# The first weight blocks of a two-layer trunk: an early constant copy on ScalarE, and no look-ahead for three blocks

## The chip, the cores and the metric

The kernel runs on one core of one Trainium2 chip, in one launch. Its time is the device time of one execution in microseconds; a lower time is better. Five engines take part: TensorE (PE in the profile; its weight loads are PEld), VectorE (DVE), ScalarE (ACT), GpSimd (POOL) and SyncE (SP, whose queue issues nearly all transfers). Host work (laying out arrays) is not in the time.

## What is computed

The reference is a decoder trunk of two layers on 512 tokens of width 1024, in float32. Layer A: a projection, pooling over windows of 2, 4, 8 and 16 positions, a grouped projection, four heads of attention to a memory of 256 tokens, an output projection, and a SwiGLU feed-forward of width 2816. Layer B: the same frame with stick-breaking attention of twelve heads in place of pooling. Only the start matters here:

```
def pool_layer(x, mem, mem_norm, norm_mix, w_in, ...):
    proj = rmsnorm(x, norm_mix) @ w_in
    u_pool, q_mem = proj[..., :POOL_WIDTH], proj[..., POOL_WIDTH:]
    ...
    mk, mv = memory_kv(mem, mem_norm, w_mem_kv)
    mem_out = memory_attention(q_mem, mk, mv)
    x = x + jnp.concatenate([grouped, mem_out], axis=-1) @ w_out
    return x + swiglu(rmsnorm(x, norm_ffn), w_gu, w_down)
```

## The kernel before

Everything is kept feature-major: a tile has 128 features on its partitions and 512 tokens along its free axis, so the residual stream is eight tiles, x0 to x7. To get nearly float32 precision at the fast rate, each operand is split in two: a high part (`xh`, `wh`) that ScalarE rounds to the type fp32r, and a remainder (`xl`, `wl`) that VectorE forms as source minus high part. A product is three matmuls of 128 x 512 into one PSUM accumulator (`mm3`): `wh` by `xh`, `wh` by `xl` and `wl` by `xh`. The norm's gain is folded into the weights: `wsplit` lets ScalarE write `wh` as weight times gain, and VectorE form `wl`.

Weights come as a stream of blocks ("bricks") of 128 x 512 in a planned order. The generator `bricks` yields them one by one, split, and starts a transfer whenever a new chunk begins. A chunk is two blocks (512 KB). Only the very first chunk is fetched as two transfers of 256 KB, with the fetch of x0 between them. `next_brick` hands the next block to a product, and keeps a queue `ahead` of up to `AHEAD` = 2 further blocks that have already been issued to the engines. One block is put into that queue before the first product is set up:

```
    net.first = lambda: fetch_x(0)
    net.ahead.append(next(net.feed))
```

The first product is the first half of the input projection (`a_in`): eight blocks, k = 0 to 7, each used for four accumulators, 12 matmuls a block. At each block `mul_in` calls `x_at(k)`, which issues the fetch of the tile x(k+1) (at k = 3: of all that remain) and the split of x(k). So what the program's order puts ahead of what on ScalarE, VectorE and the SyncE queue depends on how far `next_brick` has run ahead. The tile framework's scheduler works from that order. For the first half of the input projection it orders TensorE as well; from the memory projection on TensorE's order is fixed by hand (`in_order`).

Ahead of everything stand 20 transposes of a constant (`warm`, line 149), which occupy TensorE until data is there. The norm's statistics are squares on ScalarE (`sq`, `ssq`), sums on VectorE, and a small product `ps_ss` on TensorE; its result comes back as a row `bc` that TensorE transposes into `ps_bc`. The accumulators are first read after that.

Of the kernel before, what the change touches and what calls it, by code (L numbers as in the profile page):

```python
# [13 lines left out]
AF = mybir.ActivationFunctionType  # L14
# [46 lines left out]
AHEAD = 2  # L61
# [62 lines left out]
class Net:  # L124
    def __init__(self, ctx, tc, a, out):
        self.ctx, self.tc, self.nc, self.a, self.out = ctx, tc, tc.nc, a, out
        nc = self.nc
        self.const = ctx.enter_context(tc.tile_pool(name="const", bufs=1))
        self.wp = ctx.enter_context(tc.tile_pool(name="wp", bufs=4))
        self.tp = ctx.enter_context(tc.tile_pool(name="tp", bufs=1))  # L130
        self.pp = ctx.enter_context(tc.tile_pool(name="pp", bufs=1, space=PSUM))
        self.turn = 0
        self.now = 0.0
        self.when = {}
        self.free = {"act": 0.0, "dve": 0.0, "sp": 0.0}
        self.sides = ()
        self.banks = [0.0] * (8 - NACC)
        self.accs = deque([0.0] * NACC)
        self.gains = self.const.tile([P, 7 * KD + 6], F32, name="gains")
        nc.scalar.dma_start(self.gains, a["gains"])  # L140
        self.ident = self.const.tile([P, P], F32, name="ident")
        make_identity(nc, self.ident)
        self.ones = self.const.tile([P, 1], F32, name="ones")
        nc.gpsimd.memset(self.ones, 1.0)
        self.mhalf = self.const.tile([P, 4], F32, name="mhalf")
        nc.gpsimd.memset(self.mhalf, -0.5)
        warm = self.ps("warm")
        for i in range(WARM):
            nc.tensor.transpose(warm[:, (i % 4) * P:(i % 4 + 1) * P], self.ident, self.ident)
        self.feed, self.ahead = self.bricks(), []  # L150
        self.xh = [None] * KD
        self.xl = [None] * KD

# [42 lines left out]

    def next_brick(self, name):

        while len(self.ahead) <= AHEAD:
            nxt = next(self.feed, None)  # L200
            if nxt is None:
                break
            self.ahead.append(nxt)
        got, parts = self.ahead.pop(0)
        assert got == name
        return parts
# [893 lines left out]
```

## Time and profile before

| | us |
|---|---|
| median of three runs | 1110.95 (1109.68 to 1111.78) |
| the profiled execution, its own time | 1112.74 |
| its span, first to last instruction | 1111.0 |
| TensorE busy in the span | 1088.5 (98%) |
| VectorE busy | 677.2 (61%) |
| ScalarE busy | 498.1 (45%) |
| GpSimd busy | 77.4 (7%) |

All moments below are counted from the start of the span. Busy time of TensorE is the time in which at least one matmul is under way; a matmul's own duration (about 0.39 us for 128 x 512) is longer than the distance to the next one's start, since they are pipelined. A row of the timeline merges neighbours of one kind: start, total length, engine, line, tiles, count, and in brackets the idle time of the engine just before and what ended it.

### The profile page before, as it was taken

Reading aid. Unit: us, or ns where it says so; the run is one execution under the profiler, and the core shown is the slowest. Engines: PE = TensorE matmul, PEld = TensorE weight load, DVE = VectorE, ACT = ScalarE, POOL = GpSimd, SP = SyncE. Lnnn points to the kernel's source line nnn. Section 1 sums busy time; section 2 is a strip of 40 time slices with the busy share of each in tenths; the row PEclk is TensorE's granted clock in tenths of the full one; section 3 lists DMA queues with packets and bytes.
Section 4 is the critical chain, followed back from the end, with each engine's and each line's share of the span. In section 5 each row is a group of like instructions: output and inputs, shape, how many; then the busy total and the mean of one; then the engine's idle time right before and its main releaser. Section 6 shows DMA issues by size and latency. Waiting matters only on the chain.

```text
span 1111.0 us, 14383 instructions
## 1 busy us (share of the span) xinstructions
PE 1088.5 (98%) x5280; PEld 914.1 (82%) x5280; DVE 677.2 (61%) x1118; ACT 498.1 (45%) x911; POOL 77.4 (7%) x126
## 2 busy tenths in 40 slices
PE   9999999999999999999998999999999999999997
PEld 7987888888888888888877888778888888888887
DVE  7987766543454534565578799884563365435574
ACT  7558444332333323344786677553332243323343
POOL 0000120000000000000013143340000000000000
PEclk9999999999999999999998999999999999999999
DMA  7463222222222223223554534122222223222212
GB/s 270 140 196 103 95 94 93 99 95 95 95 95 95 97 101 104 98 95 97 135 148 111 132 100 115 58 76 95 95 96 96 99 95 107 97 95 95 95 57 76
DMA packets 39366, 117.48 MB, mean 106 GB/s; under 512 B 5120, under 2 KB 7168, under 8 KB 39296
## 3 DMA queue, kind: packets, MB, share of 16 engines
q1 hardware_dynamic: 39152, 116.54, 32.5%
q8 instruction: 41, 0.67, 0.3%
q14 instruction: 29, 0.24, 0.1%
q10 hardware_dynamic: 144, 0.03, 0.0%
HBM read 100.83 MB, written 2.10 MB: 93 GB/s over the span
## 4 chain that ended last, share of the span: by engine, by line
PE 89%; ACT 3%; DVE 3%; issue 2%; DMA 1%; POOL 0%; SPq 0%; POOLq 0%; DVEq 0%; ACTq 0%
PE acc L274 27%; PE acc L275 27%; PE acc L276 27%; PE av L646 2%; PE tp L557 1%; ACT pt L588 1%; PE zs L607 1%; PE zs L606 1%; DVE wl L224 1%; DMA wr_a_in<-in_a_in_dram 1%; ACT wh L223 1%; ACT pt L593 1%; PE ps_ss L298 0%; PE last L274 0%; PE last L275 0%
## 5 line engine op out<-in xcount | busy, mean ns | idle before, releaser
L274 PE MATMUL acc<-xh,wh 128*128 128x512 f32 x880 | 343.0, 392 | 2.0 <-DVE vs L548 1.1
L275 PE MATMUL acc<-xl,wh 128*128 128x512 f32 x880 | 343.0, 390 | 0.0
L276 PE MATMUL acc<-xh,wl 128*128 128x512 f32 x880 | 342.3, 390 | 0.0
L274 PEld LDWEIGHTS acc<-xh,wh 128*128 128x128 f32 x880 | 165.5, 188 | 35.7 <-ACT xh L233 1.7
L276 PEld LDWEIGHTS acc<-xh,wl 128*128 128x128 f32 x880 | 165.3, 188 | 34.9
L275 PEld LDWEIGHTS acc<-xl,wh 128*128 128x128 f32 x880 | 165.5, 188 | 32.9 <-DVE xl L234 0.2
L224 DVE SCALAR_TENSOR_TENSOR wl<-wr_a_gu,gains,wh 128x512 fp32r<-128x512 f32 x88 | 66.9, 761 | 110.8 <-ACT wh L223 110.8
L224 DVE SCALAR_TENSOR_TENSOR wl<-wr_b_gu,gains,wh 128x512 fp32r<-128x512 f32 x88 | 66.9, 761 | 105.5 <-ACT wh L223 105.5
L223 ACT ACTIVATE wh<-wr_a_gu,gains 128x512 fp32r<-128x512 f32 x88 | 63.7, 725 | 138.8 <-PE acc L275 111.7
L274 PE MATMUL acc<-hh,wh 128*128 128x512 f32 x320 | 124.5, 389 | 0.0
L275 PE MATMUL acc<-hl,wh 128*128 128x512 f32 x320 | 124.5, 389 | 0.0
L276 PE MATMUL acc<-hh,wl 128*128 128x512 f32 x320 | 124.3, 389 | 0.0
L223 ACT ACTIVATE wh<-wr_b_gu,gains 128x512 fp32r<-128x512 f32 x88 | 63.7, 725 | 133.3 <-PE acc L275 105.5
L276 PEld LDWEIGHTS acc<-hh,wl 128*128 128x128 f32 x320 | 60.1, 188 | 12.6
L275 PEld LDWEIGHTS acc<-hl,wh 128*128 128x128 f32 x320 | 60.1, 188 | 12.4
L274 PEld LDWEIGHTS acc<-hh,wh 128*128 128x128 f32 x320 | 60.1, 188 | 12.4
L220 DVE TENSOR_TENSOR wl<-wr_a_down,wh 128x512 fp32r<-128x512 f32 x44 | 30.4, 690 | 60.0 <-ACT wh L219 49.9
L219 ACT CAST wh<-wr_a_down 128x512 fp32r<-128x512 f32 x44 | 27.4, 623 | 72.5 <-PE acc L275 65.4
L303 POOL TENSOR_TENSOR rs<-var,mhalf 128x4 f32<-128x4 f32 (+1 forms) x7 | 6.6, 944 | 758.5 <-DVE var L301 758.5
L220 DVE TENSOR_TENSOR wl<-wr_b_down,wh 128x512 fp32r<-128x512 f32 x36 | 24.9, 690 | 49.1 <-ACT wh L219 40.9
L274 PE MATMUL acc<-mixh,wh 128*128 128x512 f32 x128 | 51.3, 401 | 1.0 <-ACT mixh L994 0.7
L275 PE MATMUL acc<-mixl,wh 128*128 128x512 f32 x128 | 50.1, 391 | 0.2 <-DVE mixl L995 0.2
(198 smaller groups left out, 1695.4 us busy)
## 6 DMA issues: line engine op xcount, KB each, us to landing
wr_a_gu<-in_a_gu_dram SPq DMA_DIRECT2D x44, 512.0 KB, 3.4
wr_b_gu<-in_b_gu_dram SPq DMA_DIRECT2D x44, 512.0 KB, 3.4
wr_a_down<-in_a_down_dram SPq DMA_DIRECT2D x22, 512.0 KB, 3.4
wr_b_qkv<-in_b_qkv_dram SPq DMA_DIRECT2D x20, 512.0 KB, 3.5
wr_b_down<-in_b_down_dram SPq DMA_DIRECT2D x18, 512.0 KB, 3.4
wr_a_out<-in_a_out_dram SPq DMA_DIRECT2D x8, 512.0 KB, 3.5
wr_b_out<-in_b_out_dram SPq DMA_DIRECT2D x8, 512.0 KB, 3.5
wr_a_in<-in_a_in_dram SPq DMA_DIRECT2D x7, 512.0 KB, 4.3
```

Of the source, the lines that this page charges most:

```text
L219: nc.scalar.copy(wh, w)
L220: nc.vector.tensor_tensor(out=wl, in0=w, in1=wh.bitcast(F32), op=ALU.subtract)
L223: nc.scalar.activation(wh[:, c0:c1], w[:, c0:c1], AF.Copy, scale=self.gain(g, k))
L224: nc.vector.scalar_tensor_tensor(out=wl[:, c0:c1], in0=w[:, c0:c1], scalar=self.gain(g, k), in1=wh.bitcast(F32)[:, c0:c1], op0=ALU.mult, o ...
L274: mm(ps, wh, xh, start=first, stop=False)
L275: mm(ps, wh, xl, start=False, stop=False)
L276: mm(ps, wl, xh, start=False, stop=last)
L557: nc.tensor.transpose(tp[:, i * P:(i + 1) * P], blk, self.ident)
L588: nc.scalar.activation(pt[:, b], z[:, b], AF.Exp, scale=sp[:, 2 * pr + i:2 * pr + i + 1], bias=mx[:, i:i + 1], accum_out=sm[:, i:i + 1])
L593: nc.scalar.activation(pt[:, b], pt[:, b], AF.Copy, scale=sm[:, i:i + 1])
L606: nc.tensor.matmul(z[:, :end], q, kh[:, :end], start=True, stop=False)
L646: self.nc.tensor.matmul(to, vv, part, start=ia == 0 and i == 0, stop=ia == nu - 1 and i == len(parts) - 1)
```

## The change

ScalarE gets one instruction more, at the front: it writes a tile of 128 x 1 as 0 times the constant `ones`. And the queue of blocks is not filled ahead for the first three calls: the condition is that one block is in hand until three have been taken, and two more after that.

```
--- before.py
+++ after.py
@@ -144,10 +144,12 @@
         nc.gpsimd.memset(self.ones, 1.0)
         self.mhalf = self.const.tile([P, 4], F32, name="mhalf")
         nc.gpsimd.memset(self.mhalf, -0.5)
+        zero = self.small("zero", 1)
+        nc.scalar.activation(zero, self.ones, AF.Copy, scale=0.0)
         warm = self.ps("warm")
...
-        self.feed, self.ahead = self.bricks(), []
+        self.feed, self.ahead, self.taken = self.bricks(), [], 0
...
     def next_brick(self, name):
 
-        while len(self.ahead) <= AHEAD:
+        self.taken += 1
+        while len(self.ahead) <= (AHEAD if self.taken > 3 else 0):
             nxt = next(self.feed, None)
```

In the built program this is what stands on ScalarE at its front. Names are tile<-source, with buffer numbers: `wr_a_in_0`, `_1`, `_2` are the chunks 0, 1, 2 of the input projection's weights (blocks 0 and 1, 2 and 3, 4 and 5). `xin` is a raw x tile. Before:

```order
L140 DMA gains_67<-in_gains_dram 128x62
L223 ACT_TABLE_LOAD
L223 ACTIVATE wh_107<-wr_a_in_0_102,gains_67 128x512
L233 CAST xh_127<-xin_104 128x512
L283 ACTIVATE ssq_143<-xin_104 128x512
L223 ACTIVATE wh_115<-wr_a_in_0_102,gains_67 128x512
L223 ACTIVATE wh_121<-wr_a_in_1_119,gains_67 128x512
L223 ACTIVATE wh_145<-wr_a_in_1_119,gains_67 128x512
L233 CAST xh_151<-xin_125 128x512
L283 ACTIVATE sq_167<-xin_125 128x512
```

And the same place in the changed kernel:

```order
L140 DMA gains_67<-in_gains_dram 128x62
L148 ACT_TABLE_LOAD
L148 ACTIVATE zero_78<-ones_74 128x1
L226 ACTIVATE wh_109<-wr_a_in_0_104,gains_67 128x512
L236 CAST xh_119<-xin_106 128x512
L286 ACTIVATE ssq_135<-xin_106 128x512
L226 ACTIVATE wh_137<-wr_a_in_0_104,gains_67 128x512
L236 CAST xh_143<-xin_117 128x512
L286 ACTIVATE sq_159<-xin_117 128x512
L286 ACTIVATE sq_186<-xin_141 128x512
L236 CAST xh_170<-xin_141 128x512
L226 ACTIVATE wh_164<-wr_a_in_1_162,gains_67 128x512
```

The activation table is loaded for the new instruction, which needs no transfer, and no longer for the first weight split. The two splits of chunk 1 have moved from ahead of the cast of x1 to behind the cast of x2.

The SyncE queue's transfers at its front, before:

```order
L189 DMA wr_a_in_0_102<-in_a_in_dram 128x512
L847 DMA xin_104<-in_x_dram 128x512
L189 DMA wr_a_in_0_102<-in_a_in_dram 128x512
L193 DMA wr_a_in_1_119<-in_a_in_dram 128x1024
L847 DMA xin_125<-in_x_dram 128x512
L847 DMA xin_149<-in_x_dram 128x512
L193 DMA wr_a_in_2_170<-in_a_in_dram 128x1024
L847 DMA xin_176<-in_x_dram 128x512
```

And in the changed kernel:

```order
L191 DMA wr_a_in_0_104<-in_a_in_dram 128x512
L850 DMA xin_106<-in_x_dram 128x512
L191 DMA wr_a_in_0_104<-in_a_in_dram 128x512
L850 DMA xin_117<-in_x_dram 128x512
L850 DMA xin_141<-in_x_dram 128x512
L195 DMA wr_a_in_1_162<-in_a_in_dram 128x1024
L850 DMA xin_168<-in_x_dram 128x512
L195 DMA wr_a_in_2_193<-in_a_in_dram 128x1024
```

Chunk 1 has moved behind the fetches of x1 and x2, and chunk 2 behind that of x3. VectorE's first 32 rows are reordered in the same sense. On TensorE a few matmuls of blocks 2 and 3 change places, and `ps_ss` stands one matmul later. Behind these places all five engines have the same rows as before, in the same order.

## Rows read from the trace of the kernel before

**Rows 1.** The page: the chain that ended last, shares of the span by engine.

```profile
PE 89%; ACT 3%; DVE 3%; issue 2%; DMA 1%; POOL 0%; SPq 0%; POOLq 0%; DVEq 0%; ACTq 0%
```

**Rows 2.** Timeline of TensorE up to the third block's first matmul.

```profile
1.55 4.53 PE L149 MATMUL warm<-ident 128*128 128x128 f32 x20 [1.55 <-POOL ident masks.py:199]
...
6.36 1.34 PE L274 MATMUL acc<-xh,wh 128*128 128x512 f32 x4 [0.28 <-ACT xh L233]
...
9.14 0.39 PE L276 MATMUL acc<-xh,wl 128*128 128x512 f32 x1
10.14 1.20 PE L274 MATMUL acc<-xh,wh 128*128 128x512 f32 x4 [0.61 <-ACT xh L233]
...
13.02 0.39 PE L274 MATMUL acc<-xh,wh 128*128 128x512 f32 x1
```

**Rows 3.** Timeline of ScalarE up to the cast of x1.

```profile
3.78 1.28 ACT L223 ACT_TABLE_LOAD   x1 [3.78 <-DMA wr_a_in<-in_a_in_dram]
...
5.70 0.60 ACT L233 CAST xh<-xin 128x512 fp32r<-128x512 f32 x1
...
8.24 1.34 ACT L223 ACTIVATE wh<-wr_a_in,gains 128x512 fp32r<-128x512 f32 x2 [0.79 <-DMA wr_a_in<-in_a_in_dram]
9.49 0.60 ACT L233 CAST xh<-xin 128x512 fp32r<-128x512 f32 x1
```

**Rows 4.** Timeline of ScalarE's and SyncE's queues: when transfers are issued.

```profile
0.80 0.41 ACTq L140 DMA_DIRECT2D gains<-in_gains_dram  x1
1.25 0.42 SPq L847 DMA_DIRECT2D xin<-in_x_dram  x1
1.72 0.42 SPq L189 DMA_DIRECT2D wr_a_in<-in_a_in_dram  x1
2.19 0.43 SPq L193 DMA_DIRECT2D wr_a_in<-in_a_in_dram  x1
2.66 0.91 SPq L847 DMA_DIRECT2D xin<-in_x_dram  x2
```

**Rows 5.** Transfers issued 0.80 to 3.61, in order: KB, us to landing.

```profile
gains<-in_gains_dram ACTq DMA_DIRECT2D x1, 31.0 KB, 3.1
...
xin<-in_x_dram SPq DMA_DIRECT2D x1, 256.0 KB, 3.7
...
wr_a_in<-in_a_in_dram SPq DMA_DIRECT2D x1, 256.0 KB, 3.9
...
xin<-in_x_dram SPq DMA_DIRECT2D x1, 256.0 KB, 6.2
...
xin<-in_x_dram SPq DMA_DIRECT2D x1, 256.0 KB, 6.8
...
wr_a_in<-in_a_in_dram SPq DMA_DIRECT2D x1, 512.0 KB, 7.6
```

**Rows 6.** Stretches: us, busy PE, PEld, DVE, ACT, POOL, PEclk, DMA, GB/s.

```profile
13.02:63.49 50.47, 50.47 (x278) 44.02 (x277) 45.44 (x90) 29.79 (x55) 2.16 (x2) 1.00 0.55 186
64.00:100.00 36.00, 32.67 (x209) 28.71 (x208) 33.05 (x72) 29.58 (x70) 0.00 (x0) 1.00 0.52 152
```

**Rows 7.** Timelines of VectorE and TensorE around the statistics.

```profile
22.51 0.69 DVE L287 TENSOR_TENSOR ssq<-ssq,sq 128x512 f32<-128x512 f32 x1
...
26.39 0.95 PE L298 MATMUL ps_ss<-ones,ssq 128*128 128x1 f32 x8
...
28.75 0.43 DVE L305 COPY bc<-rs 128x512 f32<-128x512 f32 x1 [1.21 <-POOL rs L303]
...
30.30 0.60 PE L316 MATMUL ps_bc<-ident,bc 128*128 128x128 f32 x4
30.65 0.36 PE L274 MATMUL acck<-memh,wh 128*128 128x256 f32 x1
```

**Rows 8.** TensorE's timeline at its longest stall, and the stretch around it.

```profile
598.13 0.69 PE L606 MATMUL zs<-kh,qs 128*128 128x384 f32 x1 [3.00 <-DVE atl L234]
...
597.00:605.00 8.00, 6.87 (x30) 6.51 (x31) 5.70 (x11) 4.23 (x11) 1.79 (x4) 0.57 0.44 120
```

## The prediction

> **What bounds the kernel now.** I read the page first: TensorE holds 89% of the chain that ended last [rows 1]. So an edit on ScalarE and on the order of transfers can only pay where TensorE stands still. TensorE's timeline shows where that is at the start [rows 2]. The 20 constant transposes begin at 1.55, and each has its successor 0.216 us behind it (20 of them in 4.53 us, the last 0.42 us long, so the last starts at 5.66). TensorE could take the next matmul at 5.88. It takes the first real one at 6.36, when the cast of x0 has ended (5.70 + 0.60 = 6.30) [rows 3]. The first block's twelfth matmul starts at 9.14, so the block's slot ends at 9.37. The second block starts only at 10.14, again behind a cast, that of x1 (9.49 + 0.60 = 10.09) [rows 2, 3]. The third block starts at 13.02.
>
> ScalarE's timeline tells why both casts are late [rows 3]. The table load of 1.28 us begins at 3.78, when the first weights have landed, and the weight split and the cast queue behind it. Later, ScalarE waits until 8.24 for chunk 1, does that chunk's two splits in 1.34 us, and only then casts x1. Block 1's own weights are long there by then. They were issued at 1.72 and landed 3.9 us later, at 5.62 [rows 4, 5]. So the program waits for blocks 2 and 3 before it prepares block 1's other operand.
>
> From 13.02 to 63.49 TensorE is busy 50.47 of 50.47 us [rows 6]. What it has gained by 13.02 it can keep, if its operands come as much earlier.
>
> **What the change does, part by part.** *The constant copy.* It adds one 128 x 1 instruction and moves the table load to the front, where ScalarE has nothing to do until 3.78. The copy needs only a constant that GpSimd sets before it makes the operand of the transposes (from 1.55). The load then begins behind ScalarE's one transfer issue (0.80 + 0.41 = 1.21) and ends near 2.5, well before 3.78. The first weight split starts when both its inputs are there: the weights at 3.78, the gains at 0.80 + 3.1 = 3.9 [rows 3 to 5]. It is done by about 4.65. The cast then waits for x0, which lands at 1.25 + 3.7 = 4.95 [rows 4, 5], so it ends near 5.6 and TensorE's transposes (5.88) become the later of the two. Hence the copy's 1.28 us is worth at most 6.36 - 5.88 = 0.48 us on TensorE. If that cover were gone, the cast would set the start at about 5.65.
>
> *What the clock takes back.* The first block takes 3.01 us (6.36 to 9.37). Twelve matmuls at the usual distance of 0.2275 us (from 50.47 us of steady work; a block is 2.73 us) make 2.73. The profile writes a granted clock of 1.00 there, but the transposes' 0.216 us is more than twice the 0.0875 us of the four in `ps_bc` (30.30 to 30.65) [rows 7]. So I read the start as the lower level, 1.2 GHz, and the rise as falling just behind the first real matmul. The 0.48 us that TensorE starts earlier then lie at the lower level and do half the work: minus 0.24 us.
>
> *Blocks 2 and 3 at their turn.* The fetches of x1 and x2 take the queue's slots at 2.19 and 2.66, and chunk 1 goes at about 3.14 [rows 4]. x1 then lands near 6.9: before, chunk 1 took that place and its 512 KB landed 2.6 us behind block 1's weights, so 256 KB take about 1.3 us. From its own row of before (6.2 us from issue) it would land at 8.39 at the latest. The cast takes 0.60 us, and block 1 is due on TensorE at 5.88 + 3.01 + 0.24 = 9.13, so either end is early enough. That removes the stall from 9.37 to 10.14, 0.77 us. It also removes the 0.15 us by which the second block was longer than 2.73 (13.02 - 10.14 = 2.88), since the remainder of x1 came late as well.
>
> *Chunk 1 behind x1 and x2.* This is the transfer that becomes later. The same bytes are ahead of its last one as were ahead of the last one of x2 before, which landed at 3.14 + 6.8 = 9.94 [rows 4, 5]. The longest row for 512 KB (chunk 2, 7.6 us from issue) would make it 10.74. Block 2 is due on TensorE at 9.13 + 2.73 = 11.86, and its split takes 0.72, so chunk 1 costs nothing up to 11.1. Behind the waiting split on ScalarE stand the other split, the cast of x3 and block 4's split, due from 14.6 on; they wait with it. Chunk 2 and the x tiles behind it keep their place to within one slot.
>
> *The statistics.* The last sum ends at 23.20 and `ps_ss` is issued at 26.39, so 3.2 us are spare; it now comes one matmul later and 1.2 us earlier. `bc` ends at 29.18 and `ps_bc` is issued at 30.30, with 1.1 us spare, of which the later place takes 0.23 [rows 7]. I count nothing for either.
>
> **Sum.** 0.48 - 0.24 + 0.77 + 0.15 = 1.16 us. Bounds: with the rise of the clock ahead of 5.88, blocks 0 and 1 would take 24 x 0.2275 = 5.46 us from 5.88, so block 2 would start at 11.34, 1.68 earlier; the lower bound is the second rival's 0.5. From 64 to 100 TensorE is idle 3.3 of 36 us [rows 6], in waits on ScalarE and VectorE that themselves start from TensorE's products, so I let that stretch move as a whole. The profiled execution took 1112.74 with a span of 1111.0; it should become 1111.6 and 1109.8. The median, 1.79 lower than the profiled one, becomes 1110.95 - 1.16 = **1109.8**, or 0.10% less. That is below 0.2% (2.2 us), about what a measurement of this kernel can tell from no change.
>
> **Rivals.** *1. The gain is gone later.* Some wait past 64 us may not start from TensorE but from a transfer or an engine that keeps its time. Then nothing is left: 1110.95. For it speaks that VectorE is busy 45.4 of 50.5 us ahead of that stretch; against it, that TensorE loses nothing there, so VectorE's work is in time.
>
> *2. The clock rises later than in this execution.* If the whole first block runs at the lower level (0.455 us a matmul, 5.46 us), it ends at 11.34 now and at 11.82 before. Before, x1 is then long there, and the stall that the change removes doesn't exist: only the earlier start remains, 0.48 us, 1110.5. The rows show one rise only. The Trainium skill, "TensorE: Matmul & The Clock Gate", Part 1, has the slow state as the default that activity releases, and says that the moment differs between runs of one kernel; by that, this case would occur in some executions. The rows bear the first half out (slow transposes, fast matmuls), and one execution can't show the second.
>
> *3. A fall of the clock goes away.* TensorE stands still for 3.00 us before 598.13, and the granted clock is 0.57 on average from 597 to 605: it lies at 1.2 GHz for some 6.9 us and costs 3.4 us of full clock [rows 8]. About 0.5 of that falls on the stall itself, so 3.0 us are lost. If the shifted stall no longer brings a fall, the time is 1110.95 - 1.16 - 3.0 = 1106.8. For it: standing still doesn't always bring a fall, since 3.3 us of it between 64 and 100 leave the granted clock at 1.00 [rows 6]. Against it: this stall's length doesn't change, and executions of before may differ in it already.
>
> *4. Slower: chunk 1 is late.* Two fetches of 256 KB now go ahead of it, and it could fall back further among those behind it. Block 2 then stands still, and blocks 3 to 5 are prepared behind it. Each us past 11.1 costs one; past 12.3 the gain is gone, and a landing past 14.5 (11.4 us from issue) makes it 0.2% slower, 1113.2. No row is longer than 7.6.
>
> **Chances.** Forecast (1.0 to 1.7 us gained, 1109.2 to 1110.0) 0.60; rival 1 0.12; rival 2 0.10; rival 3 0.13; rival 4 0.05. Faster by over 0.2% is rival 3 and about a fifth of the forecast, since the three runs of before are 2.1 us apart: 0.25. Slower 0.05, and within 0.2% 0.70. The range leaves out rivals 3 and 4 (0.18) and adds the spread of runs to the rest: 1107.6 to 1111.5.
>
> **What would show it.** In the profile after, the table load should start before 1.6 and no ScalarE idle time end with it. The first real matmul should start near 5.9, the second block near 9.1 and the third near 11.9, with no idle time named ahead of the second. Chunk 1 should land near 9.9, and the first split of it start there. TensorE should be fully busy to about 62.3, and the last moments should lie 1.2 us earlier. I am wrong if x1 or chunk 1 lands late enough to hold blocks 1 or 2, if a new idle row appears on TensorE before 62, or if the granted clock differs around 600.

## The result and the profile after

The change made the kernel slower: 1131.1 us (median of four runs, 1131.05 to 1133.85) against 1110.3 us before, a ratio of 1.0187 with a 95% interval of 1.0174 to 1.0200. The forecast was 1109.8, in a range of 1107.6 to 1111.5.

The profiled execution after has a span of 1132.1 us. At the start it looks much as forecast. These are rows of the timeline after, of ScalarE first and then of TensorE; they answer to [rows 2, 3]:

```profile
1.24 1.28 ACT L148 ACT_TABLE_LOAD   x1 [1.24 <-PEq L1091]
...
4.68 0.61 ACT L236 CAST xh<-xin 128x512 fp32r<-128x512 f32 x1
...
8.85 0.62 ACT L236 CAST xh<-xin 128x512 fp32r<-128x512 f32 x1 [1.92 <-DMA xin<-in_x_dram]
...
5.73 1.99 PE L277 MATMUL acc<-xh,wh 128*128 128x512 f32 x4
...
9.52 0.76 PEld L277 LDWEIGHTS acc<-xh,wh 128*128 128x128 f32 x4 [0.37 <-ACT xh L236]
9.52 1.20 PE L277 MATMUL acc<-xh,wh 128*128 128x512 f32 x4
...
12.42 0.86 PE L277 MATMUL acc<-xh,wh 128*128 128x512 f32 x3
```

The table load is out of the way, the first real matmul starts at 5.73 in place of 6.36, and the third block at 12.42 in place of 13.02. So 0.6 us are won by then. All the same the span is 21.1 us longer. TensorE doesn't stand still for them. Its row on the page after, and the three rows of its largest product:

```profile
PE 1109.7 (98%) x5280; PEld 915.1 (81%) x5280; DVE 677.9 (60%) x1118; ACT 498.9 (44%) x912; POOL 77.6 (7%) x126
...
L277 PE MATMUL acc<-xh,wh 128*128 128x512 f32 x880 | 348.1, 398 | 1.1 <-DVE vs L551 1.1
L278 PE MATMUL acc<-xl,wh 128*128 128x512 f32 x880 | 347.0, 395 | 0.0
L279 PE MATMUL acc<-xh,wl 128*128 128x512 f32 x880 | 346.6, 395 | 0.0
```

TensorE is busy 21.2 us longer with the same 5280 matmuls (1088.5 before), and idle before these products for no longer than then. The reader should see this first: the bound engine has the same work and no more waits, but more busy time. So each piece takes longer. To see how much, count pieces in a stretch where nothing else happens. From 200 to 500 us both kernels run the feed-forward of layer A without a gap. This is that stretch before (first row, 1325 matmuls in 300 us) and after (second row):

```profile
200.00:500.00 300.00, 300.00 (x1325) 248.39 (x1325) 148.87 (x227) 99.16 (x154) 0.00 (x0) 1.00 0.28 97
```

```profile
200.00:500.00 300.00, 300.00 (x1293) 243.21 (x1292) 142.98 (x218) 95.17 (x147) 0.00 (x0) 1.00 0.27 95
```

300 / 1325 is 226.4 ns a matmul, 300 / 1293 is 232.0: 5.6 ns more, or 2.5%, at a granted clock of 1.00 in both. The page counts 3 x (880 + 320 + 128) = 3984 matmuls of 128 x 512 with split weights. 3984 x 5.6 ns is 22.3 us. Less the 0.6 us won at the start, that makes 21.7 us, where the spans differ by 21.1. It looks closer than it is, for the two profiles also differ in TensorE's clock near 600 us. Before, the granted clock was 0.57 from 597 to 605 [rows 8]; after, it was 0.89 in this stretch:

```profile
605.00:620.00 15.00, 11.76 (x71) 10.59 (x70) 12.19 (x22) 10.55 (x23) 4.67 (x10) 0.89 0.50 120
```

That is some 6.9 us at 1.2 GHz before and some 3.3 after, worth some 1.8 us to the profile after. With it the sum is some 19.9 us, and about 1.2 of the 21.1 stay without an account.

Not every matmul is slower. From the view that groups instructions by line and shape, whole span, before:

```profile
L275 PE MATMUL acc<-hl,wh 128*128 128x512 f32 x320 | 124.5, 389 | 0.0
...
L275 PE MATMUL last<-hl,xh 128*128 128x256 f32 x64 | 18.1, 284 | 0.0
...
L275 PE MATMUL acck<-meml,wh 128*128 128x256 f32 x32 | 9.0, 283 | 0.0
...
L607 PE MATMUL zs<-kb,qs 128*128 128x512 f32 x12 | 4.7, 393 | 0.0
```

and after:

```profile
L278 PE MATMUL acc<-hl,wh 128*128 128x512 f32 x320 | 126.3, 395 | 0.0
...
L278 PE MATMUL last<-hl,xh 128*128 128x256 f32 x64 | 18.1, 284 | 0.0
...
L278 PE MATMUL acck<-meml,wh 128*128 128x256 f32 x32 | 9.0, 282 | 0.0
...
L610 PE MATMUL zs<-kb,qs 128*128 128x512 f32 x12 | 4.7, 392 | 0.0
```

The products of 128 x 512 with `wh` or `wl` as weights went from 389 to 395 ns. The scores `zs` and the last block's product `last` didn't change, and both their operands lie in the same memory pool, the work pool. That points to where tiles lie, but it is a hint and no more. `last` is 128 x 256, and products of that length didn't get slower even with `wh` as weights and a work tile as the moving operand (`acck`, 283 and 282 ns). So the loss is one of the 128 x 512 products, and only the 12 matmuls of `zs` speak for the place; the experiments have to decide. In the built programs, `small("zero", 1)` is the first tile of the work pool `tp`. It has four buffers of 32 bytes, so every work tile behind it begins 128 bytes further along its partition: `xh` at byte 68736 in place of 68608, `hh` at 115840 in place of 115712. The weight tiles `wh` and `wl`, in the pool ahead, stay at 35840 and 44032.

### The profile page after: what moved, and what is told of

Read it like the earlier page. It is cut to its first block, busy times and chain, and to the rows that moved or that the text cites. A ratio compares the mean times of both kernels' runs of the same rounds, so it can differ in the third digit from the quotient of the medians.

```text
span 1132.1 us, 14384 instructions
## 1 busy us (share of the span) xinstructions
PE 1109.7 (98%) x5280; PEld 915.1 (81%) x5280; DVE 677.9 (60%) x1118; ACT 498.9 (44%) x912; POOL 77.6 (7%) x126
## 4 chain that ended last, share of the span: by engine, by line
PE 91%; ACT 3%; DVE 2%; issue 2%; DMA 1%; POOL 0%; SPq 0%; POOLq 0%; DVEq 0%; ACTq 0%
PE acc L277 28%; PE acc L279 27%; PE acc L278 27%; PE av L649 2%; PE tp L560 1%; ACT pt L591 1%; PE zs L610 1%; PE zs L609 1%; ACT pt L596 0%; PE ps_ss L301 0%; PE last L277 0%; PE last L278 0%; PE warm L151 0%; PE last L279 0%; PE acck L279 0%
## 5 line engine op out<-in xcount | busy, mean ns | idle before, releaser
L277 PE MATMUL acc<-xh,wh 128*128 128x512 f32 x880 | 348.1, 398 | 1.1 <-DVE vs L551 1.1
L278 PE MATMUL acc<-xl,wh 128*128 128x512 f32 x880 | 347.0, 395 | 0.0
L279 PE MATMUL acc<-xh,wl 128*128 128x512 f32 x880 | 346.6, 395 | 0.0
```

Source lines behind the costliest of these rows:

```text
L277: mm(ps, wh, xh, start=first, stop=False)
L278: mm(ps, wh, xl, start=False, stop=False)
L279: mm(ps, wl, xh, start=False, stop=last)
```

## The experiments

Theory A: the tile's place does it. Theory B: the new order or the earlier start puts TensorE into a slower state. Theory C: the early copy or table load does it. All times are compared with runs of the kernel before on the same chip (1110.2 to 1111.6 in the median).

**The whole change, but no tile moves.** The copy goes into unused bytes behind a constant. The order on all five engines is that of the changed kernel.

```
-        self.mhalf = self.const.tile([P, 4], F32, name="mhalf")
-        nc.gpsimd.memset(self.mhalf, -0.5)
+        self.mhalf = self.const.tile([P, 5], F32, name="mhalf")
+        nc.gpsimd.memset(self.mhalf[:, :4], -0.5)
+        nc.scalar.activation(self.mhalf[:, 4:5], self.ones, AF.Copy, scale=0.0)
...
-        while len(self.ahead) <= AHEAD:
+        self.taken += 1
+        while len(self.ahead) <= (AHEAD if self.taken > 3 else 0):
```

> The whole change, with every engine's instructions in the order of the changed kernel, but the copy is written into 4 unused bytes behind the constant mhalf, so that no tile moves in memory. Theory A (the new tile moves every later work tile by 128 bytes, and that makes the matmuls of 128 x 512 slower by 5 to 6 ns each): the distance between matmuls is back at 227 ns, and the time is 1.0 to 1.7 us below the kernel before, some 1109. Theory B (the new order or the earlier start puts TensorE into a slower state for the whole run): the distance stays at 232 and the time near 1131. Theory C (the early copy or table load does it): the same as B, near 1131.

Measured: 1109.3 us, ratio 0.9985 (0.9975 to 0.9995). The chosen stretch holds 1325 matmuls again:

```profile
200.00:500.00 300.00, 300.00 (x1325) 248.51 (x1324) 149.13 (x228) 99.49 (x155) 0.00 (x0) 1.00 0.29 97
```

B and C fall: order, copy and table load are all there, and the matmuls are fast. The change's own idea gains 0.15%. Its start on TensorE:

```profile
5.73 1.34 PE L276 MATMUL acc<-xh,wh 128*128 128x512 f32 x4
...
8.72 1.07 PE L276 MATMUL acc<-xh,wh 128*128 128x512 f32 x4
...
11.44 0.84 PE L276 MATMUL acc<-xh,wh 128*128 128x512 f32 x3
```

The third block starts 1.58 us earlier than before (13.02), which agrees with the ratio (0.0015 x 1111 = 1.7 us).

**The look-ahead alone.** No copy, no tile.

```
-        while len(self.ahead) <= AHEAD:
+        self.taken += 1
+        while len(self.ahead) <= (AHEAD if self.taken > 3 else 0):
```

> The look-ahead edit alone: no copy, no new tile, every tile where it was before. Theory A: 227 ns, and a gain of 0.4 to 1.2 us, since the table load again stands behind the first weights but the cast of x1 no longer stands behind chunk 1; near 1109.5. Theory B: near 1131. Theory C: near 1110.

Measured: 1110.0 us, ratio 0.9987 (0.9978 to 0.9996), 1325 matmuls in the stretch. So the order alone brings a gain; what the copy adds can't be told from nothing by these times, since the intervals overlap. In the profile the first real matmul stands at 6.45 here and at 5.73 with the copy, the third block at 12.06 and at 11.44. By these rows 0.62 of the 1.58 us at the third block came with the copy.

**The copy alone,** in its own tile.

```
+        zero = self.small("zero", 1)
+        nc.scalar.activation(zero, self.ones, AF.Copy, scale=0.0)
```

> The copy alone with its tile, look-ahead as before: the work tiles stand 128 bytes later. Theory A: 232 ns and near 1131 to 1132, the first product starting near 5.7 us and the second block still waiting behind chunk 1. Theory B: 227 ns and near 1110. Theory C: near 1131.

Measured: 1133.3 us, ratio 1.0199 (1.0184 to 1.0213), 1293 matmuls in the stretch. The slower matmuls come with the copy's line and without the order.

**Neither edit, only bytes.**

```
+        pad = self.tp.tile([P, 32], F32, tag="pad", name="pad", bufs=1)
+        nc.gpsimd.memset(pad, 0.0)
```

> Neither edit: the kernel before with a tile of 128 bytes per partition put at the front of the work pool, which GpSimd fills once and nothing reads. Theory A: 232 ns, some 21 us slower than before, near 1132. Theories B and C: as before, near 1110.

Measured: 1134.9 us, ratio 1.0212 (1.0196 to 1.0228), 1292 matmuls:

```profile
200.00:500.00 300.00, 300.00 (x1292) 243.21 (x1291) 142.82 (x218) 94.16 (x145) 0.00 (x0) 1.00 0.29 95
```

128 bytes that nothing reads cost what the change cost. Theory A stands; the next runs ask what about the place it is.

**The same bytes ahead of weights and work tiles.**

```
+        pad = self.const.tile([P, 32], F32, name="pad")
+        nc.gpsimd.memset(pad, 0.0)
```

> The kernel before with the 128 bytes put ahead of everything that is large: the split weights wh and wl move by 128 bytes too, and their distance to the work tiles is what it was. Theory A1 (what counts is the place of the moving tile itself, a multiple of 512 bytes before and 128 beyond one after): 232 ns, near 1132. Theory A2 (what counts is the distance between the two operands of a matmul): 227 ns, near 1110.

Measured: ratio 1.0005 (0.9993 to 1.0017), and 1325 matmuls:

```profile
200.00:500.00 300.00, 300.00 (x1325) 248.42 (x1324) 148.87 (x227) 99.00 (x154) 0.00 (x0) 1.00 0.29 97
```

All large tiles lie 128 bytes off their old place, and nothing is slower. A1 falls: it isn't the place of the moving tile by itself, but how it lies to the large tiles ahead of it, the weights among them.

**The bytes behind xh and xl.** Ahead of the first `ssq` tile, which follows them in the pool:

```
+        if not hasattr(self, "pad"):
+            self.pad = self.tp.tile([P, 32], F32, tag="pad", name="pad", bufs=1)
+            nc.gpsimd.memset(self.pad, 0.0)
```

> The kernel before with the 128 bytes put behind the tiles xh and xl and ahead of all later work tiles. So xh and xl stay and hh, hl, mixh, mixl and the rest move. Both A1 and A2: matmuls with xh or xl as the moving tile at 227 ns, those with hh, hl, mixh and mixl at 232 or 233; 960 + 384 such matmuls by 5.7 ns are 7.7 us, so near 1118. A third theory, that the whole program gets slower by where it lies, would slow all or none.

Measured: ratio 1.0079 (1.0050 to 1.0108), 1120.1 us, some 2 us more than forecast. The same stretch by line, both sorts of product inside one execution:

```profile
L275 PE MATMUL acc<-xl,wh 128*128 128x512 f32 x275 | 107.0, 389 | 0.0
...
L275 PE MATMUL acc<-hl,wh 128*128 128x512 f32 x162 | 64.0, 395 | 0.0
```

`xl` hasn't moved and is fast, `hl` has and is slow. That excludes every cause that acts on the program as a whole.

**Other distances.** 32 and 64 bytes at the front of the work pool of the kernel before; then 192 and 96 in the kernel of the first experiment, at the same place. This is the edit for 32 bytes; the others differ in the number of columns (16, 48 and 24 in place of 8).

```
+        pad = self.tp.tile([P, 8], F32, tag="pad", name="pad", bufs=1)
+        nc.gpsimd.memset(pad, 0.0)
```

> The kernel before with a tile of 32 bytes at the front of the work pool. If any step off the place of before costs the same, 232 ns and near 1132; if the cost grows with the step, a quarter of 21 us, near 1116; if what counts is a boundary coarser than 32 bytes that a row of 2048 bytes straddles once more, as with 128: near 1132.

> The same with 64 bytes. Near 1132 if any step costs the same, near 1121 if the cost grows with the step, near 1110 if every other step is free.

> The whole change with the copy in the unused bytes (as in the first run) and the work tiles moved by 192 bytes. If the cost goes by the distance between the operands in steps of 64 bytes that repeat each 128, as 64 (9 us) would say, near 1118; if it grows with the distance, above 1131; if there is a better place than the old one, below 1109.

> The same with 96 bytes: near 1135 if every distance that is not a multiple of 64 costs what 32 did (25 us), between 1118 and 1131 if it lies between its neighbours 64 and 128.

| work tiles moved against the weights by | ratio (interval) | matmuls in 200 to 500 us |
|---|---|---|
| 0 (first experiment) | 0.9985 (0.9975 to 0.9995) | 1325 |
| 32 | 1.0227 (1.0197 to 1.0258) | 1288 |
| 64 | 1.0078 (1.0049 to 1.0107) | 1312 |
| 96 | 1.0208 (1.0179 to 1.0238) | 1287 |
| 128 (neither edit) | 1.0212 (1.0196 to 1.0228) | 1292 |
| 192 | 1.0212 (1.0176 to 1.0248) | 1287 |

The rows for 0, 96 and 192 have the change's own gain of 0.15% in their ratio, the others don't; the counts of matmuls can be compared as they are. The cost neither grows with the distance nor is it the same for all, and 192 isn't 64 again, as I had thought possible. None of these places is better than the old one. At 64 bytes the three matmuls of a product differ, in the same stretch:

```profile
L276 PE MATMUL acc<-xh,wh 128*128 128x512 f32 x276 | 108.8, 394 | 0.0
L278 PE MATMUL acc<-xh,wl 128*128 128x512 f32 x277 | 108.6, 392 | 0.0
L277 PE MATMUL acc<-xl,wh 128*128 128x512 f32 x276 | 107.1, 388 | 0.0
```

All three have moving tiles 64 bytes off, against their own weights and against the next ones alike, as `wh` and `wl` both keep their places. So this distance alone doesn't set what one matmul costs.

**The bytes between wh and wl.** To see whether a matmul's own weights count or those that are loaded beside it.

```
+            if not hasattr(self, "pad"):
+                self.pad = self.wp.tile([P, 32], F32, tag="pad", name="pad", bufs=1)
+                nc.gpsimd.memset(self.pad, 0.0)
             wl = self.wp.tile([P, cols], F32R, tag="wl", name="wl", bufs=4)
```

> The kernel before with the 128 bytes put between wh and wl: wl and all work tiles move, wh stays. So the distance of the moving tile to wl is what it was and that to wh is 128 bytes off. TensorE's order is wh by xh, wh by xl, wl by xh. If a matmul is slowed by the place of its own weights, the two with wh are slow (some 232 ns) and the one with wl is at 227: two thirds of 21 us, near 1124. If it is slowed by the load of the next matmul's weights, which runs beside it, wh by xl (whose next weights are wl) is at 227 and the other two are slow: the same time, and other lines. If what counts were the distance of the moving tile to the tiles that ScalarE and VectorE write meanwhile, no third would stand apart.

Measured: ratio 1.0222 (1.0192 to 1.0251), and no third is fast:

```profile
L279 PE MATMUL acc<-xh,wl 128*128 128x512 f32 x280 | 111.3, 397 | 0.0
L278 PE MATMUL acc<-xl,wh 128*128 128x512 f32 x279 | 110.2, 395 | 0.0
L277 PE MATMUL acc<-xh,wh 128*128 128x512 f32 x279 | 109.6, 393 | 0.0
```

Both of my theories for this run fail. In each of the three matmuls either the own weights or the next ones are `wh`, which lies 128 bytes off, so that both might count. But the matmul with `wl`, whose own place fits, is the longest. The outcome is also the one named for the third theory, the tiles that ScalarE and VectorE write meanwhile. The trace of this run speaks against that one. For 1.71 us neither of the two engines runs, as the first row shows (VectorE and ScalarE 0.00), and TensorE goes on as slowly. The other two rows are its first and last start in this time:

```profile
385.41:387.12 1.71, 1.71 (x9) 1.36 (x8) 0.00 (x0) 0.00 (x0) 0.00 (x0) 1.00 0.40 108
```

```profile
385.44 0.39 PE L277 MATMUL acc<-hh,wh 128*128 128x512 f32 x1
...
387.07 0.40 PE L278 MATMUL acc<-hl,wh 128*128 128x512 f32 x1
```

Seven distances take 1.63 us, 233 ns each. It is so in the whole stretch from 200 to 500 us, counted from the starts in the trace: matmuls during which neither engine runs stand 233.3 ns apart, all others 233.3 as well, and those during which no transfer's packet is under way either, again 233.3. So the loss needs no other engine and no transfer. Between own weights and next weights the run settles nothing.

## Why the prediction was wrong

**The step that failed** is the first sentence on the copy: "It adds one 128 x 1 instruction and moves the table load to the front". I costed the instruction and left out that `small("zero", 1)` also takes memory, at the front of the pool in which every moving operand lies. With it fell the sentence under the bound, "What it has gained by 13.02 it can keep": I took each later matmul to last as it did, and every block's length, the 2.73 us, rests on that. The runs showed in its place 5.6 ns more from one matmul of 128 x 512 to the next (226.4 to 232.0), some 22 us over 3984 of them. No rival had this mechanism. Rival 4, the slower one, had a late chunk 1; that isn't what happened, since chunk 1 is issued at 3.14 and lands 7.5 us later, near 10.6, ahead of the 11.1 that I had named as its limit. Rival 1, the gain gone later, came nearest, but looked for a wait where there is none.

Rival 3, the fall of the clock near 600 us, did bear on the profiles, and one of my signs of being wrong (a granted clock that differs there) came true. These rows are of the first experiment and of the last:

```profile
590.00:605.00 15.00, 12.37 (x70) 10.91 (x69) 12.90 (x22) 9.06 (x19) 2.93 (x7) 0.89 0.59 149
```

```profile
590.00:630.00 40.00, 37.66 (x226) 33.05 (x225) 36.17 (x60) 29.24 (x60) 13.97 (x28) 1.00 0.41 107
```

So the time at 1.2 GHz was some 6.9 us in the profile before, some 3.3 in those of the change and of the first experiment, and none in that of the last run. TensorE's longest stall there was 3.0, 3.2, 2.6 and 2.3 us, so its length alone doesn't decide. Whether the change shortens the fall or executions of one kernel differ in it, one profile of each can't say. It explains none of the loss: where the clock is 1.00 throughout, the matmuls are as slow.

**What was right, by the steps at the start.** *The copy* frees the first matmul: 5.73, forecast "near 5.9" (the transposes let it start 0.15 us ahead of my 5.88). *The first weight split* waits for the gains: 4.05, forecast 3.9. *The stall ahead of block 1* (0.77) is gone in the first experiment, where block 1 follows at 8.72 without idle time. In the profile of the change, 0.37 us of TensorE's weight loads wait there again. x1 landed 6.6 us from issue, near 8.8, later than my latest, 8.39; in the first experiment, with the same transfers in the same order, it took 4.8 and landed near 7.0, as estimated. In three more runs with this order of transfers it took 5.0, 5.2 and 5.4 us; in the last two of these the x tiles had moved as well, so the place doesn't explain the 6.6. I can put it down to nothing but the transfers' own spread. *The clock at the start:* the first four matmuls took 1.83 us (5.73 to 7.56) in the profile of the change and 1.18 (5.73 to 6.91) in the first experiment. That is 0.46 and 0.30 us each, where 0.23 is usual. The granted clock is written as 1.00 in both, so that I can only read it from the distances, as in the prediction: 0.46 is twice the usual, the lower level of 1.2 GHz for all four in the one, and for a part of them in the other. The record of the granted clock that the traces keep fits: it begins, at full clock, at 7.52 us in the one and at 6.11 in the other. Read so, the moment of rival 2 does differ between executions. *The sum* of 1.16 us was 1.58 in the profile of the first experiment, inside its bounds (0.5 to 1.68), and 1.7 (0.6 to 2.8) by its ratio, at the upper one. What it fell short by is the 0.15 us at the first matmul and the 0.24 that I took off for the clock: the first block took 2.99 us there (5.73 to 8.72), against 3.01 before, so the clock took back nothing more than before. *Statistics and later stretches:* by the ratio, the gain arrives at the end when the tiles stay in place. The profile's span shows more, 3.3 us (1107.7 for 1111.0), of which the clock near 600 us is worth some 1.8.

**What is shown and what is open.** Shown: 128 bytes without any use slow the matmuls as the change does; the change without them is faster than before; moved together with the weights they cost nothing; and a product of 128 x 512 slows if its moving tiles are shifted against the weights, with no other engine at work, while products of 128 x 256 don't. Open: why. That the reads of moving tile and weights get in each other's way is a guess that the relative place suggests; no run here shows the reads, and the last one doesn't fit a simple form of it. Nor do the six distances tried give a rule.

## What to carry to other kernels

A new tile, however small, is an edit to the place of every tile behind it; put it at the end of the last pool or into unused bytes of an old one, and compare the tiles' places before and after as you compare the instructions' order. When a kernel gets slower and its bound engine is busier with the same instructions, count that engine's instructions over a stretch without waits: if the count falls, look for what makes one instruction longer, not for a wait. And to value a small edit on its own, keep the places equal: here 0.15% faster stood against 1.9% slower for the same order of instructions.

## What the hardware showed that I had not expected

The distance between matmuls of 128 x 512 in fp32r, 226.4 ns with the work tiles in their old place to the weights, is 232 to 233 ns when they lie 32, 96, 128 or 192 bytes off, and 228.7 (300 / 1312) at 64 bytes off, at a granted clock of 1.00 throughout. The products of 128 x 256 that I compared didn't slow (283 and 282 ns with `wh` as weights, 128 bytes off). And one transfer of 256 KB, the same in order and size, landed 4.8 to 5.4 us from its issue in four executions and 6.6 in a fifth.
